# Output gate and silu path of a head side by side in 512 streamed columns

## The chip, the core and the metric

One Trainium2 chip, of which one core runs the kernel. The metric is device time in microseconds (us), the median of several executions. TensorE (PE) does the matmuls; in the profile PEld is its loading of stationary operands, which overlaps with the streaming of others. VectorE is DVE, ScalarE is ACT, GpSimd is POOL, and SP issues the DMA transfers. PSUM, where matmuls accumulate, has banks of 512 fp32 columns for each of 128 partitions.

## The reference, cut to what matters

```python
def reference(x, norm_g, w_in, ..., w_out, final_norm_g):   # x: 1 x 2048 x 1024
    u = rmsnorm(x, norm_g)
    proj = einsum('bsd,de->bse', u, w_in)        # 1024 -> 8200 columns
    (q, k, v, o_pre, z_m, i_pre, f_pre,          # 1024 columns each, gates 4 each
     glu_a, glu_g, z_c) = split(proj)
    hm = mlstm_chunkwise(q, k, v, i_pre + b_i, f_pre + b_f)  # 4 heads of 256
    hm = sigmoid(o_pre) * hm
    hm = headwise_rmsnorm(hm) * mh_norm_g * silu(z_m)
    c = causal_depthwise_conv31(glu_a * sigmoid(glu_g)) + conv_b
    c = silu(layernorm(c)) * silu(z_c)
    return rmsnorm(x + concat(hm, c) @ w_out, final_norm_g)
```

## The kernel before

The 2048 tokens are worked in two halves of 1024 (`hf` 0 and 1). In each half the input projection runs as a row of units (function `unit`, line 321): a unit is one pass over the 1024 input features in 8 k-steps, with four PSUM banks as output, and the pool `gm` has five banks, so a unit starts on the one that the unit before it didn't use. Every product is three matmuls, since both operands are split into a high and a low part (`hi*hi + hi*lo + lo*hi`).

The units of a half follow in the order of the list `seq`: two groups of conv input (`g`), then for each head `v`, `o` (output gate), `z` (silu path), `q`, `k`, and two more `g`; at the end four `c`. Units of kind "fm" (`g`, `q`, `k`, `c`, line 336) hold the weights stationary and stream 512 tokens. Units of kind "tm2" (`v`, `o`, `z`, line 343) hold a tile of 128 tokens stationary and stream 256 weight columns; two token tiles share one bank. Units of kind "tm" (line 350) stream weights too, one token tile to a bank; the output projection at the end uses them with 512 columns.

Weights come by DMA into tiles `wr` of 512 KB (`w_load`, two buffers) and are split in two by `w_prep_`: a copy on ACT (line 221) and a subtraction on POOL (line 222), into four buffers `w`, three tiles ahead of use (`WAHEAD`). For `o` and `z` a split tile holds two k-steps of 256 columns, and starts 48 words into its buffer (`ODD`). So a head's `o` and `z` take 4 loads and 8 splits.

`ev_o` evacuates the output gate with two sigmoids of 256 columns to a bank (line 438), and `ev_z` the silu path with two sigmoids (line 450) and two products on DVE (line 451). Evacuations and weight splits are issued at a high priority (`first_hand`).

The order of instructions on each engine comes from a planner, which places them by priority, readiness and modelled costs. Work behind the units is handed out by two queues at each k-step: `ml_slot` gives out the chunks of the mLSTM of the head before, 26 slots from the unit after `k` on, and `pump` gives out DVE work by credit: the 31 taps of each convolution block (line 787, kept in program order), and in the second half the layernorm of the first.

Of the kernel before, what the change touches and what calls it, by code (L numbers as in the profile page):

```python
# [14 lines left out]
F32 = mybir.dt.float32  # L15
F32R = mybir.dt.float32r
AF = mybir.ActivationFunctionType
ALU = mybir.AluOpType

P = 128  # L20
# [4 lines left out]
HD = 256  # L25
# [14 lines left out]
def hybrid_block_kernel(  # L40
# [12 lines left out]
    nc = tc.nc  # L53
# [5 lines left out]
    PAD, ODD = 8, 48  # L59

    def pool(name, bufs, **kw):
        return ctx.enter_context(tc.tile_pool(name=name, bufs=bufs, **kw))
# [6 lines left out]
    ozp = pool("ozp", 4)  # L69
# [107 lines left out]
    def ml_slot():  # L177
        gate_step()
        if mlq:
            for fn in mlq.popleft():  # L180
                fn()

    def ml_drain():
        while mlq:
            ml_slot()

    def first_hand():
        return tc.high_priority(offset=HP)
# [3 lines left out]
    wsrc = []  # L192
# [4 lines left out]
    def w_load(j):  # L197
        ap, n, _ = wsrc[j]
        r = rp.tile([P, 1056], F32, tag="raw", name=f"wr{j}")
        raws[j] = (r, n)  # L200
        if j > 0:
            with first_hand():
                nc.sync.dma_start(r[:, : 2 * n], ap)

    def w_first(half):
        r, n = raws[0]
# [20 lines left out]
    def w_advance(i):  # L227

        while wstate["prep"] <= min(i + WAHEAD, 2 * len(wsrc) - 1):
            k = wstate["prep"]  # L230
            while wstate["raw"] <= min(k // 2 + 1, len(wsrc) - 1):
                w_load(wstate["raw"])
                wstate["raw"] += 1
            w_prep(k)
            wstate["prep"] += 1
# [6 lines left out]
    rstd = {}  # L242
# [68 lines left out]
    def m_kc(b, kp):  # L311
        with first_hand():
            for j in range(kp, min(kp + 2, 8)):
                if (b, j) not in mraw:
                    m_load(b, j)
            split((f"m{b}", kp), mraw[b, kp])
# [4 lines left out]
    def unit(kind, nk, kpt, ncol, opnd, evac, step_us=2.6, hook=None, toks=None, ntail=0):  # L321


        ps = [gm.tile([P, 512], F32, tag="gm", name=f"gm_{wpos[0]}_{i}") for i in range(4)]
        base = wpos[0]

        def products(kc, i):
            wh, wl = wtile[base + kc // kpt]
            o = (kc % kpt) * ncol
            ah, al = opnd(kc)  # L330
            first, last = kc == 0, kc == nk - 1
            for pi, (wt, at) in enumerate(((wh, ah), (wh, al), (wl, ah))):
                st, sp_ = first and pi == 0, last and pi == 2
                if kind == "fm":
                    cb, tb = i % 2, i // 2
                    nc.tensor.matmul(  # L336
                        ps[i], wt[:, o + cb * P : o + (cb + 1) * P], at[:, tb * 512 : (tb + 1) * 512],
                        start=st, stop=sp_,
                    )
                elif kind == "tm2":  # L340
                    for t2 in range(2):
                        t = 2 * i + t2
                        nc.tensor.matmul(  # L343
                            ps[i][:, t2 * 256 : (t2 + 1) * 256], at[:, t * P : (t + 1) * P],
                            wt[:, o : o + ncol],
                            start=st and t2 == 0, stop=sp_, skip_group_check=True,
                        )
                else:
                    t = toks[i]
                    nc.tensor.matmul(  # L350
                        ps[i][:, :ncol], at[:, t * P : (t + 1) * P], wt[:, o : o + ncol],
                        start=st, stop=sp_,
                    )

        tail = nk - ntail
        for kc in range(tail):
            w_advance(base + kc // kpt)
            if hook is not None:
                hook(kc)
            for i in range(4):  # L360
                products(kc, i)
            ml_slot()
            pump(step_us * PUMP)
        for kc in range(tail, nk):
            w_advance(base + kc // kpt)
        wpos[0] += nk // kpt
        for i in range(4):
            for kc in range(tail, nk):
                products(kc, i)
            if hook is not None:  # L370
                for kc in range(tail + i * ntail // 4, tail + (i + 1) * ntail // 4):
                    hook(kc)
            with first_hand():
                evac(i, ps[i])
            for _ in range(ntail // 4):
                ml_slot()
                pump(step_us * PUMP)


    q_t, k_t, v_t, oz_t = {}, {}, {}, {}  # L380
# [50 lines left out]
            )  # L431
        return f

    def ev_o(hf, h):
        def f(i, ps):
            oz_t[h, i] = ozp.tile([P, 2, 2, HD], F32, tag="oz", name=f"oz_{hf}_{h}_{i}")
            for j in range(2):
                nc.scalar.activation(
                    oz_t[h, i][:, 0, j], ps[:, j * HD : (j + 1) * HD], AF.Sigmoid,
                    scale=rstd["c"][:, 2 * i + j : 2 * i + j + 1],  # L440
                )
        return f

    def ev_z(hf, h):
        def f(i, ps):
            t = oz_t[h, i]
            for j in range(2):
                pv = ps[:, j * HD : (j + 1) * HD]
                rc = rstd["c"][:, 2 * i + j : 2 * i + j + 1]
                nc.scalar.activation(t[:, 1, j], pv, AF.Sigmoid, scale=rc)  # L450
                nc.vector.scalar_tensor_tensor(  # L451
                    out=t[:, 1, j], in0=pv, scalar=rc, in1=t[:, 1, j], op0=ALU.mult, op1=ALU.mult
                )
        return f

    def gates(hf, gt):
# [450 lines left out]
    WID = {}  # L907
    n = 0
# [12 lines left out]
    for hf in range(2):  # L921
        s = [("g", 0)]
        for h in range(NH):
            s += [("v", h)] + ([("g", 1)] if h == 0 else []) + [("o", h), ("z", h), ("q", h), ("k", h)]
            if h < 3:
                s += [("g", 2 * h + 2), ("g", 2 * h + 3)]
        s += [("c", j) for j in range(4)]
        seq.append(s)
        for u in s:
            if u == ("v", 0):  # L930
                for _ in range(2):
                    for g in range(2):
                        wsrc.append((wv0[g], 528, 0))
            else:
                for g in range(2):
                    wsrc.append((wu[WID[u], g], 512, ODD if u[0] in "ozv" else 0))
    for b in range(4):
        for nn in range(2):
            for g in range(8):
# [18 lines left out]
    for hf in range(2):  # L958
        gt = gp.tile([P, NCH, 8], F32, tag="g_gt", name=f"gt{hf}")
        key = f"u{hf}"  # L960

        def opnd(kc, key=key):
            return uh[key, kc], ul[key, kc]

        s = seq[hf]
        hold[0] = 10**6
        for ui, (nm, i) in enumerate(s):
            hook = None
            if ui == len(s) - 1:
                if hf == 0:  # L970
                    def hook(kc):
                        if kc >= 1:
                            u_kc(1, kc - 1)
                else:
                    def hook(kc):
                        if kc >= 1:
                            m_kc(0, kc - 1)
            if nm == "g":
                unit("fm", 8, 2, 256, opnd, ev_glu(hf, i), hook=hook)
            elif nm == "c":  # L980
                unit("fm", 8, 2, 256, opnd, ev_zc(hf, i), hook=hook)
            elif nm == "q":
                unit("fm", 8, 2, 256, opnd, ev_q(hf, i), hook=hook)
            elif nm == "k":
                unit("fm", 8, 2, 256, opnd, ev_k(hf, i), hook=hook)
                mlstm(hf, i)
            elif nm == "o":
                unit("tm2", 8, 2, 256, opnd, ev_o(hf, i), hook=hook)
            elif nm == "z":
                unit("tm2", 8, 2, 256, opnd, ev_z(hf, i), hook=hook)  # L990
            elif i > 0:
                unit("tm2", 8, 2, 256, opnd, ev_v(hf, i), hook=hook)
            else:
                for g in range(2):
                    unit("tm", 8, 2, 264, opnd, ev_v0(hf, g, gt), step_us=1.35, toks=[4 * g + i for i in range(4)])
                gq.append([0, gates(hf, gt)])
                gate_step()
        if hf == 0:
            u_kc(1, 7)
            u_rstd(1)  # L1000
        else:
            m_kc(0, 7)
        if hf == 1:
            ml_drain()
            drain()
        for blk in range(4):
            layernorm(hf, blk)
# [36 lines left out]
    for b in range(4):  # L1044
        if b == 2:
            drain()
        for nn in range(2):
            hook = None
# [78 lines left out]
```

## Time and profile before

| what | value |
|---|---|
| median of 3 runs | 2008.14 us (2007.59 to 2011.28) |
| the profiled execution | 2014.07 us |
| its span, first to last instruction | 2012.4 us |
| mean granted TensorE clock | 0.993 |
| PE busy | 1975.9 us, 98% |
| DVE busy | 1445.4 us, 72% |
| ACT busy | 827.7 us, 41% |
| POOL busy | 792.3 us, 39% |

The profile is that of one execution. An engine's busy time is the union of its instructions' times; matmuls overlap one another in it. A wait is put down to the instruction that released it.

### The profile page before, as it was taken

How to read it: one execution, taken by the hardware profiler on the slowest of the kernel's cores; microseconds unless marked ns; L12 is line 12 of the kernel's file. 1: busy time of each engine (PE TensorE's matmuls, PEld its weight loads, DVE VectorE, ACT ScalarE, POOL GpSimd, SP SyncE). 2: the span in 40 equal slices, each digit the busy share in tenths (PEclk: the TensorE clock that was granted, in tenths of full speed). 3: DMA queues.
4: the chain of work that ended last, by engine and by line, in shares of the span. 5: the costliest groups of instructions: out<-in, count | busy, mean ns of one | idle time of the engine just before them, and what ended most of it. 6: DMA issues, size and time to landing. Idle time of an engine off the chain costs nothing.

```text
span 2012.4 us, 29602 instructions
## 1 busy us (share of the span) xinstructions
PE 1975.9 (98%) x11562; PEld 1744.7 (87%) x11562; DVE 1445.4 (72%) x1915; ACT 827.7 (41%) x1703; POOL 792.3 (39%) x740
## 2 busy tenths in 40 slices
PE   8999999999999999999999999999999999999998
PEld 7998998899899888888889879988998887788887
DVE  6598887699679765557799998977896658733221
ACT  5233432442343246545345224424523555543332
POOL 4632432333243332433333324333432236565564
PEclk9999999999999999999999999999999999999999
DMA  4121121212122233335211211211221566766452
GB/s 151 64 69 53 58 74 43 63 49 74 42 69 74 74 110 125 113 126 162 85 53 53 69 42 59 74 53 53 64 74 53 163 220 200 248 231 231 155 190 95
DMA packets 85836, 204.10 MB, mean 101 GB/s; under 512 B 7296, under 2 KB 40256, under 8 KB 85696
## 3 DMA queue, kind: packets, MB, share of 16 engines
q1 hardware_dynamic: 85696, 202.21, 30.6%
q8 instruction: 91, 1.49, 0.3%
q14 instruction: 49, 0.40, 0.1%
HBM read 159.15 MB, written 43.03 MB: 100 GB/s over the span
## 4 chain that ended last, share of the span: by engine, by line
PE 73%; DVE 18%; DMA 3%; issue 2%; ACT 2%; POOL 0%; SPq 0%; POOLq 0%; DVEq 0%; ACTq 0%
PE gm L336 32%; PE gm L343 18%; PE gm L350 16%; DVE y L787 11%; PE num L601 3%; PE kv L601 2%; PE sk L627 1%; DMA ly<-ysc 1%; DVE sm L302 1%; DMA wr<-in_wo 1%; PE mt L714 1%; DVE ly L844 1%; DMA ysc<-y 1%; PE sk L631 1%; ACT ly L881 0%
## 5 line engine op out<-in xcount | busy, mean ns | idle before, releaser
L222 POOL TENSOR_TENSOR w<-wr,w 128x512 fp32r<-128x512 f32 (+1 forms) x392 | 603.1, 1543 | 878.2 <-ACT w L221 859.4
L336 PE MATMUL gm<-u_u,w 128*128 128x512 f32 x3840 | 908.6, 392 | 0.7 <-DVE u_u L293 0.6
L336 PEld LDWEIGHTS gm<-u_u,w 128*128 128x128 f32 x3840 | 712.5, 188 | 143.2 <-DVE u_u L293 1.3
L787 DVE SCALAR_TENSOR_TENSOR y<-c,vec,y 128x1024 f32<-128x1024 f32 x480 | 714.5, 1489 | 9.7
L343 PE MATMUL gm<-w,u_u 128*128 128x256 f32 x4224 | 521.9, 281 | 5.7 <-DVE oz L451 3.4
L343 PEld LDWEIGHTS gm<-w,u_u 128*128 128x128 f32 x4224 | 505.8, 190 | 7.6 <-DVE oz L451 3.6
L221 ACT CAST w<-wr 128x512 fp32r<-128x512 f32 (+1 forms) x392 | 241.4, 620 | 591.6 <-PE gm L336 200.2
L350 PE MATMUL gm<-w,u_m 128*128 128x512 f32 x1536 | 355.0, 392 | 3.1 <-POOL w L222 1.9
L350 PEld LDWEIGHTS gm<-w,u_m 128*128 128x128 f32 x1536 | 289.1, 189 | 64.2 <-POOL w L222 2.8
L281 DVE TENSOR_TENSOR u_m<-mr,u_m 128x1024 fp32r<-128x1024 f32 x32 | 47.2, 1475 | 77.7 <-ACT u_m L280 77.7
L1019 DVE TENSOR_TENSOR ht<-gm,ht 128x512 f32<-128x512 f32 x32 | 21.5, 687 | 112.2 <-PE gm L350 112.2
L700 POOL TENSOR_TENSOR ss<-ss,nhalf 128x1 f32<-128x1 f32 x64 | 55.5, 867 | 111.9 <-ACT sq L699 111.3
L633 DVE SCALAR_TENSOR_TENSOR w<-sk,rs,ee 128x128 f32<-128x128 f32 x64 | 22.0, 344 | 81.6 <-PE sk L631 79.1
L601 PE MATMUL kv<-v,kw 128*128 128x258 f32 x360 | 74.3, 291 | 0.6 <-DVE cs L666 0.4
L666 DVE SCALAR_TENSOR_TENSOR cs<-cs,g_so,kv 128x258 f32<-128x258 f32 x112 | 53.3, 476 | 25.1 <-PE kv L601 24.7
L639 ACT ACTIVATE kw<-sk,g_wa 128x256 fp32r<-128x256 f32 x60 | 28.3, 472 | 81.7 <-DVE w L633 81.6
L719 ACT ACTIVATE mo<-mt,vec 128x128 f32<-128x128 f32 x128 | 39.7, 362 | 52.3 <-PE mt L714 52.1
L601 PEld LDWEIGHTS kv<-v,kw 128*128 128x128 f32 x360 | 56.9, 190 | 3.2 <-DVE cs L666 0.6
L408 DVE SCALAR_TENSOR_TENSOR v<-gm,rs,v 128x256 fp32r<-128x256 f32 x64 | 29.5, 475 | 33.4 <-ACT v L407 33.4
L699 ACT ACTIVATE sq<-hm 128x257 bf16<-128x257 f32 x64 | 26.9, 420 | 64.6 <-DVE hm L694 64.4
L761 POOL TENSOR_TENSOR c<-c,g 128x512 f32<-128x512 f32 x32 | 40.9, 1284 | 30.4 <-ACT g L760 27.6
L350 PE MATMUL gm<-w,u_u 128*128 128x264 f32 x384 | 50.8, 294 | 0.0
(200 smaller groups left out, 1818.0 us busy)
## 6 DMA issues: line engine op xcount, KB each, us to landing
wr<-in_wu SPq DMA_DIRECT2D x123, 512.0 KB, 3.6
wr<-in_wo SPq DMA_DIRECT2D x64, 512.0 KB, 3.6
mr<-mixs SPq DMA_DIRECT2D x32, 512.0 KB, 4.6
ysc<-y SPq DMA_DIRECT2D x16, 512.0 KB, 2.6
mixs<-mo SPq DMA_DIRECT2D x32, 256.0 KB, 2.1
zsc<-zc SPq DMA_DIRECT2D x32, 256.0 KB, 2.1
ly<-ysc SPq DMA_DIRECT2D x16, 512.0 KB, 5.2
lz<-zsc SPq DMA_DIRECT2D x16, 512.0 KB, 6.0
```

What stands on the lines that cost most here:

```text
L221: nc.scalar.copy(hi, s)
L222: nc.gpsimd.tensor_tensor(out=lo, in0=s, in1=hi.bitcast(F32), op=ALU.subtract)
L281: nc.vector.tensor_tensor(out=l_, in0=src, in1=h_.bitcast(F32), op=ALU.subtract)
L336: nc.tensor.matmul(ps[i], wt[:, o + cb * P : o + (cb + 1) * P], at[:, tb * 512 : (tb + 1) * 512], start=st, stop=sp_,)
L343: nc.tensor.matmul(ps[i][:, t2 * 256 : (t2 + 1) * 256], at[:, t * P : (t + 1) * P], wt[:, o : o + ncol], start=st and t2 == 0, stop=sp_, s ...
L350: nc.tensor.matmul(ps[i][:, :ncol], at[:, t * P : (t + 1) * P], wt[:, o : o + ncol], start=st, stop=sp_,)
L601: nc.tensor.matmul(ps, x_, y_, start=start and i == 0, stop=stop and i == 2)
L666: nc.vector.scalar_tensor_tensor(out=cs[:, d], in0=cs[:, d], scalar=so[:, h, c : c + 1], in1=kv[:, :VW], op0=ALU.mult, op1=ALU.add,)
L700: nc.gpsimd.tensor_tensor(out=ss, in0=ss, in1=nhalf[:, 0:1], op=ALU.pow)
L719: nc.scalar.activation(mo[:, d, (cc % 2) * P : (cc % 2 + 1) * P], mt[:, d * P : (d + 1) * P], AF.Identity, scale=col(V_MG, 2 * h + d),)
L761: nc.gpsimd.tensor_tensor(out=c[:, sl], in0=c[:, sl], in1=g, op=ALU.mult)
L787: tc.keep_in_program_order(nc.vector.scalar_tensor_tensor(out=y, in0=c[:, j + i * H2 : j + (i + 1) * H2], scalar=col(V_CW, b * CW + j), in1=y,
```

## The change

The units `o` and `z` of a head become two units `oz` of kind "tm", each with four token tiles. A weight tile now holds one k-step of 256 `o` columns and 256 `z` columns side by side, so a matmul streams 512 columns into a whole bank that belongs to one token tile. Both units go through all the weights of the head, so they are loaded and split twice. A load is made of two DMA transfers, one from the `o` weights and one from the `z` weights, interleaved in the destination. A bank is evacuated by one sigmoid over both halves and one product on DVE for the `z` half. The offset `ODD` is left for `v` alone.

```diff
@@ w_load
-                nc.sync.dma_start(r[:, : 2 * n], ap)
+                if isinstance(ap, tuple):
+                    rv = r[:, :1024].rearrange("p (a b c) -> p a b c", a=2, b=2)
+                    for k in range(2):
+                        nc.sync.dma_start(rv[:, :, k, :], ap[k])
+                else:
+                    nc.sync.dma_start(r[:, : 2 * n], ap)
@@ evacuation
-    def ev_o(hf, h):
...
-    def ev_z(hf, h):
...
+    def ev_oz(hf, h, g):
+
         def f(i, ps):
+            t = 4 * g + i
+            if t % 2 == 0:
+                oz_t[h, t // 2] = ozp.tile([P, 2, 2, HD], F32, tag="oz", name=f"oz_{hf}_{h}_{t // 2}")
+            o = oz_t[h, t // 2][:, :, t % 2, :]
+            rc = rstd["c"][:, t : t + 1]
+            nc.scalar.activation(o, ps.rearrange("p (a b) -> p a b", a=2), AF.Sigmoid, scale=rc)
+            nc.vector.scalar_tensor_tensor(
+                out=o[:, 1], in0=ps[:, HD : 2 * HD], scalar=rc, in1=o[:, 1], op0=ALU.mult, op1=ALU.mult
+            )
         return f
@@ order of units and of weights
-            s += [("v", h)] + ([("g", 1)] if h == 0 else []) + [("o", h), ("z", h), ("q", h), ("k", h)]
+            s += [("v", h)] + ([("g", 1)] if h == 0 else []) + [("oz", h), ("q", h), ("k", h)]
...
+            elif u[0] == "oz":
+                for _ in range(2):
+                    for g in range(2):
+                        for k in (0, 2):
+                            wsrc.append((
+                                tuple(wu[WID[nm, u[1]], g][:, k : k + 2, :] for nm in "oz"), 512, 0
+                            ))
             else:
                 for g in range(2):
-                    wsrc.append((wu[WID[u], g], 512, ODD if u[0] in "ozv" else 0))
+                    wsrc.append((wu[WID[u], g], 512, ODD if u[0] == "v" else 0))
...
-            elif nm == "o":
-                unit("tm2", 8, 2, 256, opnd, ev_o(hf, i), hook=hook)
-            elif nm == "z":
-                unit("tm2", 8, 2, 256, opnd, ev_z(hf, i), hook=hook)
+            elif nm == "oz":
+                for g in range(2):
+                    unit("tm", 8, 1, 512, opnd, ev_oz(hf, i, g), hook=hook, toks=[4 * g + j for j in range(4)])
```

## Rows read from the trace of the kernel before

**Rows 1.** The page: busy time of the engines, and DVE in 40 slices.
```profile
PE 1975.9 (98%) x11562; PEld 1744.7 (87%) x11562; DVE 1445.4 (72%) x1915; ACT 827.7 (41%) x1703; POOL 792.3 (39%) x740
...
DVE  6598887699679765557799998977896658733221
```

**Rows 2.** Groups by line and shape: busy us, mean ns | idle before, releasers.
```profile
L787 DVE SCALAR_TENSOR_TENSOR y<-c,vec,y 128x1024 f32<-128x1024 f32 x480 | 714.5, 1489 | 9.7
L222 POOL TENSOR_TENSOR w<-wr,w 128x512 fp32r<-128x512 f32 x376 | 577.9, 1541 | 859.0 <-ACT w L221 844.5 <-DVE dn L687 9.4 <-DVE c1l L592 4.6
...
L221 ACT CAST w<-wr 128x512 fp32r<-128x512 f32 x376 | 231.4, 619 | 577.4 <-PE gm L336 189.3 <-PE gm L350 114.0 <-issue 111.8
...
L450 ACT ACTIVATE oz<-gm,rs 128x256 f32<-128x256 f32 x64 | 27.9, 478 | 37.6 <-PE gm L343 23.4 <-DVE oz L451 14.2
...
L438 ACT ACTIVATE oz<-gm,rs 128x256 f32<-128x256 f32 x64 | 25.8, 486 | 9.8 <-PE gm L343 6.9 <-DVE hm L706 2.8
```

**Rows 3.** Timeline of PE, three undisturbed stretches: start us, us, instructions.
```profile
284.28 23.40 PE L343 MATMUL gm<-w,u_u 128*128 128x256 f32 x205
...
635.74 22.66 PE L343 MATMUL gm<-w,u_u 128*128 128x256 f32 x191
...
1786.67 131.63 PE L350 MATMUL gm<-w,u_m 128*128 128x512 f32 x580
```

**Rows 4.** Windows, line 343 alone: the sum over the eight o-and-z stretches.
```profile
sum 399.00, PE 374.36 PEld 365.13; mean PE 46.79 PEld 45.64
```

**Rows 5.** Waits of PE: who for whom, us in total, times, longest us.
```profile
PE gm L343 <- DVE oz L451: 3.4, 1, 3.4
...
PE gm L350 <- POOL w L222: 1.9, 2, 1.2
...
PE gm L343 <- ACT oz L438: 1.7, 2, 1.1
```

**Rows 6.** Timeline of PE, first head of the second half, z.
```profile
928.26 5.92 PE L343 MATMUL gm<-w,u_u 128*128 128x256 f32 x26 [3.42 <-DVE oz L451]
```

**Rows 7.** Windows: length, busy us of each engine, granted clock, DMA share, GB/s.
```profile
881.30:937.20 55.90, 51.40 (x408) 50.76 (x407) 35.54 (x43) 28.38 (x50) 15.28 (x10) 0.94 0.49 153
...
985.00:1206.00 221.00, 209.67 (x1266) 185.79 (x1265) 211.60 (x263) 79.81 (x181) 75.07 (x67) 0.98 0.17 54
...
1830.90:1874.40 43.50, 43.50 (x194) 36.05 (x193) 10.80 (x10) 13.22 (x26) 26.83 (x24) 1.00 0.62 216
```

**Rows 8.** The chain that ended last, 970 to 1195 us: two taps, and its end.
```profile
977.71 1.29 DVE y L787
...
980.35 2.21 DVE y L787
...
1192.67 2.56 PE gm L336 x6
```

**Rows 9.** Timeline of all engines where z of head 3 ends, first half.
```profile
656.31 0.47 ACT L450 ACTIVATE oz<-gm,rs 128x256 f32<-128x256 f32 x1 [2.87 <-PE gm L343]
...
658.23 8.12 PE L336 MATMUL gm<-u_u,w 128*128 128x512 f32 x35
...
658.84 0.87 DVE L451 SCALAR_TENSOR_TENSOR oz<-gm,rs,oz 128x256 f32<-128x256 f32 x2
...
659.49 1.29 POOL L222 TENSOR_TENSOR w<-wr,w 128x512 fp32r<-128x512 f32 x1 [4.29 <-ACT w L221]
659.63 2.23 DVE L787 SCALAR_TENSOR_TENSOR y<-c,vec,y 128x1024 f32<-128x1024 f32 x1
```

**Rows 10.** DMA issues: KB each, median us to landing.
```profile
wr<-in_wu SPq DMA_DIRECT2D x123, 512.0 KB, 3.6
...
mixs<-mo SPq DMA_DIRECT2D x32, 256.0 KB, 2.1
```

**Rows 11.** Source views of lines 451 and 787: ns min/median/max, first and last start.
```profile
L451 DVE SCALAR_TENSOR_TENSOR oz<-gm,rs,oz x64: 467/475/485, 134.5 to 1490.4; 128x256 f32<-128x256 f32 x64
...
L787 DVE SCALAR_TENSOR_TENSOR y<-c,vec,y x480: 1250/1285/2415, 82.6 to 1579.0; 128x1024 f32<-128x1024 f32 x160
```

More of the change, by code (lines that the diff above doesn't have):

```diff
@@ L432, in ev_v0 @@
         return f
-    def ev_o(hf, h):
+    def ev_oz(hf, h, g):
         def f(i, ps):
[L436 to L442, printed above, removed]
-    def ev_z(hf, h):
[L445 to L453, printed above, removed]
+            t = 4 * g + i
[7 more added lines that the diff above has]
+            )
         return f
```

## The prediction

> **What bounds the kernel now.** I read the page's busy line and slices first [rows 1]. TensorE (PE) is busy 98% of the span, VectorE (DVE) 72%, the others under half; so the end is set by the stream of matmuls, and DVE matters only where its slices stand at 9 and PE waits for it. The list of groups [rows 2] then gives durations of what an edit on ACT, POOL and DVE costs. A matmul's own duration is no use as a price, because matmuls overlap: the price is the step from start to start, which the timeline of PE gives where one line runs undisturbed [rows 3]. A row of n matmuls lasts n-1 steps and the last one's own time (0.28 us for 256 columns, 0.39 us for 512). So the 205 of the first row step by (23.40-0.28)/204 = 113.3 ns, the 191 of the second by (22.66-0.28)/190 = 117.8 ns (three more z units have that same row), and the 580 of 512 columns, streamed weights against stationary tokens just as the change wants it, by (131.63-0.39)/579 = 226.7 ns.
>
> **The stream of the output gate and silu units (o, z).** Before, a head takes 2 x 192 matmuls of 256 columns, after, 2 x 96 of 512: the same columns. At the faster old step a head is 384 x 113.3 = 43.5 us, at the slower 384 x 117.8 = 45.2 us; after, 192 x 226.7 = 43.5 us. Eight heads (four in each half) so gain between 0 and 8 x 1.7 = 13.9 us. The slow step is in four of the five undisturbed z stretches, while o and the disturbed z units are mixed with other matmuls; I take five eighths of the way, about 8.5 us. As a check, line 343 is busy 374.4 us in the eight stretches together [rows 4], against 8 x 43.5 = 348: 26 us is the most that could go, with every wait and every tail between pieces.
>
> The Trainium skill, "TensorE: Matmul & The Clock Gate", section "Back-to-back issue gap", gives a warm isolated matmul N/2.4 + 2.5 ns. By it 256 columns would step by 109.2 and 512 by 215.8 ns, and an estimate from that page for the gain is 1536 x 2.6 = 4 us in place of 8.5. Both traced steps are longer than the page's, so the sum goes by the rows.
>
> **The waits of PE in these units.** PE waited 3.4 and 1.7 us there for the evacuations of lines 451 and 438 [rows 5], nearly all in the first head of the second half. The long one was followed by 26 matmuls in 5.92 us [rows 6], (5.92-0.28)/25 = 226 ns each where 117 is usual: the granted clock of that stretch is 0.94 [rows 7], so part of it ran at the lower of the clock's two levels, 1.2 GHz, for another 2.8 us. That is 7.9 us in all. It is caused by layernorm work of the first half on ACT and DVE, which the change leaves in place; I credit 2 us, with 0 and 7.9 as ends.
>
> **Weights.** Each head's o and z weights are now split twice, once for each unit: 8 more copies on ACT and 8 more subtractions on POOL in a head, 64 in all: 64 x 0.619 = 40 us of ACT and 64 x 1.541 = 99 us of POOL [rows 2]. Neither engine is near full, and the output projection already runs at this rate: 16 splits in 43.5 us, with PE busy 43.5 of 43.5 [rows 7]. So supply costs nothing where DVE and ACT are quiet; where they weren't, PE waited 1.9 us for POOL in the whole projection [rows 5]. The loads double too, 32 to 64 transfers' worth, each now in two issues of 256 KB in 1 KB pieces. The nearest row of that form is the store of mo, 2.1 us from issue to landing, against 3.6 us for one 512 KB load [rows 10]; two are 2.1 to 4.2 us plus an issue. A pair of weight tiles lasts 2 x 12 x 0.2267 = 5.4 us, and three tiles are ready ahead, so the transfer stays covered. If SP held one up behind a layernorm store, that cover would shrink from the 17 us of now to 8. Cost taken: 0.
>
> **Evacuation.** The o units took 8 sigmoids of 0.486 us, the z units 8 of 0.478 [rows 2]; 8 of 512 wide take their place, between 0.48 and 0.96 us each, near the 0.619 of the 512-wide copy. ACT is relieved by some 2 to 3 us a head, off the path. DVE keeps its 8 products of 0.475 us [rows 11], but now the first unit's banks wait for DVE as well, where o's waited for ACT alone. What stands in front is a convolution tap. In [rows 9] the first sigmoid of z ends at 656.78 and its DVE product starts at 658.84, 2.1 us late; q streamed from 658.23 on without a pause, because with five banks it starts on the free one and can go up to eight k-steps deep on four ready weight tiles. In the new pair a tile holds one k-step: four tiles give 4 x 3 x 0.2267 = 2.7 us on the free bank. The first bank is finished 2.04 us before the unit ends, and sigmoid, lateness and product take 0.6 + 2.1 + 0.5 = 3.2 us, so it is back 1.2 us into the next unit, within the 2.7. One lengthened tap (2.2 us) in front of it makes 3.4 and PE waits 0.7. Ends: 0, and 8 x 2.2 = 17.6 us; I take 0.3 us a head, 2.4 us.
>
> **What POOL does to DVE.** A tap alone takes about 1.285 us, and the mean of all is 1.489 [rows 2, 11]. In [rows 9] the tap of 659.63 meets a POOL subtraction of 659.49 and takes 2.23; so also the chain's 2.21 against its neighbour's 1.29 [rows 8]. One collision costs DVE 0.92 us; spread over the splits that run beside taps, 480 x (1.489-1.285) = 98 us over the 376 + 16 - 128 = 264 splits ahead of the projection is 0.37 each. Eight more a head are 3.0 to 7.4 us of DVE. In most heads DVE has room for it in the k unit. It hasn't from 985 to 1206 us, where it is busy 211.6 of 221 us [rows 7] and where the chain runs tap by tap from 974 until PE takes over at 1192 [rows 8]: the second half's second head. There I take 5 us, and the 1.1 us of faster stream in that head is lost, being off the path. Ends: 0, and 14.7 us if the next head carries the lateness too.
>
> The Trainium skill, "GPSIMD Engine Reference", section "Key points", says that GpSimd shares its SBUF interfaces with VectorE and contends with instructions that have two SBUF inputs. The trace agrees: the tap, with two, spans 1.250 to 2.415 us, while the product of line 451, with one input in PSUM, stays within 0.467 and 0.485 [rows 11]. That rule speaks against the change.
>
> **Sum.** -8.5 (stream) -2 (waits) +2.4 (banks) +5 +1.1 (DVE) = -2 us. The profiled execution took 2014.07 us (span 2012.4 and 1.7 around it), 5.9 us over the median 2008.14 of the three timed runs; so 2012.1 in its own terms, 2006 on the median.
>
> **Rivals.** *The stream's gain is kept.* The new order takes the waits away and DVE finds room: -8.5 - 7.9 = -16.4, 1992 us. For it: in most o and z units PE never waits now. Against: the DVE chain of 218 us.
> *DVE becomes the bound.* The place is the second half, heads two and three; the price 14.7 us for 16 collisions at 0.92, 8 x 0.7 us at the banks, less 8.5 us of stream: +12, 2020 us. It decides once a head's extra DVE time exceeds what k leaves idle. For it: 211.6 of 221 busy. Against: not every split meets a tap. This is the contention rule of the Trainium skill at full price.
> *The stream is not faster at all.* If the old step is mostly 113.3 ns, what is left of the sum is -2 + 2.4 + 5 = +5.4: 2013.5 us. For it: the first row of [rows 3]. Against: the four rows at 117.8.
>
> **How the numbers follow.** A measurement tells about 0.2% (4 us) from no change. Forecast (2006, own range 2000 to 2012): 0.42, of which 0.14 faster, 0.22 same, 0.06 slower. Gain kept: 0.22, faster. DVE the bound: 0.25, of which 0.23 slower, 0.02 same. No faster stream: 0.11, of which 0.05 same, 0.06 slower. So faster 0.36, same 0.29, slower 0.35. Half of each outer case lies beyond its centre, so the range goes from 1991 to 2022.
>
> **What would show it.** Rows of 512-column matmuls in the new units stepping by 227 ns; some 43.5 us for a pair that nothing interrupts; 64 more splits; taps of 2.2 us at nearly twice the rate inside the pairs; PE waiting for line 451's successor at the middle of a pair by under 1 us; the DVE chain after 974 longer by about 5 us. Wrong if PE waits for POOL's weights inside the pairs, if mid-pair waits reach 2 us, or if the planner's new order moves waits in stages that the diff doesn't touch by more than these few microseconds.

## The result and the profile after

The changed kernel takes 2080.19 us (2078.94 to 2081.9, four runs) against 2007.87 for the kernel before beside it: a ratio of 1.0358, 95% interval 1.0341 to 1.0375. It is 72 us slower, where 2 us faster was forecast, and far beyond the range's upper end of 2022. Its profiled execution has a span of 2077.7 us and a mean granted clock of 0.977 (before: 2012.4 and 0.993).

In the changed kernel the copy of a weight split is line 226 and the subtraction 227, the matmuls of `oz` are line 355, those of `q` and `k` 341, of `v` 348, sigmoid and product of `oz` 447 and 448, the taps 784, and the evacuation of a `g` unit 753 (c) and 756 (gate).

The page of the changed kernel, busy time, DVE's and the clock's slices, three groups and two rows of DMA issues (to set against [rows 1, 2, 10]):
```profile
PE 1982.1 (95%) x10026; PEld 1676.1 (81%) x10026; DVE 1496.5 (72%) x1915; ACT 853.4 (41%) x1702; POOL 906.8 (44%) x804
...
DVE  6698887799689766467789977996886766833122
...
PEclk9999999999999999979998999999999999999999
...
L227 POOL TENSOR_TENSOR w<-wr,w 128x512 fp32r<-128x512 f32 (+1 forms) x456 | 721.0, 1589 | 807.9 <-ACT w L226 791.8
...
L784 DVE SCALAR_TENSOR_TENSOR y<-c,vec,y 128x1024 f32<-128x1024 f32 x480 | 750.5, 1564 | 9.6
...
wr<-in_wu SPq DMA_DIRECT2D x91, 512.0 KB, 3.5
wr<-in_wu SPq DMA_DIRECT2D x130, 256.0 KB, 3.0
```
PE's busy time has hardly moved (6 us more), and its share has fallen from 98 to 95%: the added time is PE standing still. DVE does the same 1915 instructions in 51 us more. POOL has its 64 more splits.

The waits of PE in the changed kernel (against [rows 5]):
```profile
PE lv L856 <- DVE lq L825: 20.4, 3, 11.9
PE gm L341 <- DVE oz L448: 13.3, 7, 4.5
PE gm L355 <- DVE oz L448: 9.5, 6, 3.4
...
PE lm L833 <- DVE ls L825: 7.0, 3, 5.3
PE bc_l L274 <- DVE dg_l L270: 4.9, 4, 1.6
PE gm L355 <- POOL w L227: 4.0, 5, 1.2
```
Two things are new: PE waits 22.8 us in all for the DVE product of `oz` (second and third row), and 32 us for layernorm's own steps (the `lv`, `lm` and `bc_l` rows). The latter mislead on their own: a tiny matmul of layernorm is named because nothing else on PE can run. Of the 4.0 us for POOL's split weights, 1.9 are in the output projection, as before [rows 5]; some 2 us are new, inside the pairs.

Where the time goes shows best unit by unit. The table is worked out from the timelines of PE: from the first matmul of a head's `o` (or `oz`) to the first of its `q`, in us, for the four heads of each half (1.0 to 1.3 is the first half, 2.0 to 2.3 the second). The runs below `after` are the experiments of the next section.

| kernel | 1.0 | 1.1 | 1.2 | 1.3 | 2.0 | 2.1 | 2.2 | 2.3 |
|---|---|---|---|---|---|---|---|---|
| before | 47.0 | 47.5 | 49.9 | 49.9 | 55.9 | 52.7 | 48.1 | 48.1 |
| after | 50.6 | 48.7 | 50.2 | 50.2 | 90.3 | 72.5 | 50.9 | 47.5 |
| x5_pool | 53.4 | 48.5 | 50.4 | 50.4 | 58.3 | 59.9 | 51.4 | 48.7 |
| x1_depth | 46.3 | 47.0 | 48.9 | 48.9 | 92.6 | 65.0 | 46.5 | 48.7 |
| x9_nosub | 46.3 | 47.5 | 50.2 | 50.2 | 91.0 | 70.1 | 45.5 | 46.7 |
| x11_depth_dg | 46.3 | 47.0 | 48.9 | 48.9 | 48.7 | 67.0 | 46.3 | 48.7 |

Two pairs carry most of it: the first head of the second half, 34 us longer, and the second, 20 us longer. The first half as a whole loses 11.0 us. Between the two long pairs 12 us are made up again, and from the last head's `q` to the `c` units another 7 are lost. (The profiled execution before is 6 us over its median, so these sums come to 65 us and not to 72.)

The timeline of PE in the first of them, and below it DVE's and POOL's of the same stretch (against [rows 6], where PE streams on):
```profile
892.27 7.42 PE L355 MATMUL gm<-w,u_u 128*128 128x512 f32 x32
...
899.88 1.19 PE L355 MATMUL gm<-w,u_u 128*128 128x512 f32 x4
...
903.61 0.67 PE L833 MATMUL lm<-ls,ones 128*128 128x256 f32 x2 [0.45 <-DVE ls L825]
916.18 0.98 PE L856 MATMUL lv<-invd,lq 128*128 128x1 f32 x4 [11.90 <-DVE lq L825]
...
938.76 7.55 PE L355 MATMUL gm<-w,u_u 128*128 128x512 f32 x24
```
```profile
936.77 0.42 DVE L270 TENSOR_TENSOR dg_l<-ident,lrs 128x256 f32<-128x256 f32 x1 [0.88 <-POOL lrs L859]
937.11 1.28 DVE L756 TENSOR_TENSOR g<-gm,rb 128x512 f32<-128x512 f32 x2
```
```profile
893.22 1.55 POOL L227 TENSOR_TENSOR w<-wr,w 128x512 fp32r<-128x512 f32 x1 [4.87 <-ACT w L226]
...
941.63 2.28 POOL L227 TENSOR_TENSOR w<-wr,w 128x512 fp32r<-128x512 f32 x1
```
PE does 32 + 4 = 36 matmuls of `oz` and then none for 37.7 us. Thirty-six is 3 banks x 4 weight tiles x 3 products: the unit has used up every split tile on every bank that it holds. Its fourth bank, and one for the unit after it, are still full with the gates of the `g` unit before, which DVE takes out at 937.11, right behind the third diagonal of layernorm in its order. Until then no weight tile can be released, since the fourth bank has still to use all four, and so POOL splits nothing from 893 to 941. In the kernel before the gates come out just as late, at 938.99; there four tiles hold all eight k-steps of a unit, and PE went on with what it had.

The second head has the same, behind other work. PE of the changed kernel:
```profile
1109.62 5.17 PE L355 MATMUL gm<-w,u_u 128*128 128x512 f32 x22
...
1115.20 0.73 PE L355 MATMUL gm<-w,u_u 128*128 128x512 f32 x2
...
1134.09 4.46 PE L355 MATMUL gm<-w,u_u 128*128 128x512 f32 x12 [1.38 <-DVE v L413]
1139.65 3.04 PE L355 MATMUL gm<-w,u_u 128*128 128x512 f32 x12 [1.11 <-DVE c L753]
```
22 + 2 = 24 is two banks by 4 tiles by 3. Then the third bank comes when DVE has evacuated `v`, the fourth with a `c` of the `g` unit, each good for 12 more.

Windows of the changed kernel over the two pairs and over the stretch of the DVE chain (columns and the old stretches in [rows 7]):
```profile
892.30:982.60 90.30, 56.93 (x235) 43.52 (x234) 62.04 (x77) 48.70 (x79) 30.93 (x23) 0.79 0.48 154
985.00:1206.00 221.00, 202.48 (x1023) 170.18 (x1022) 194.82 (x230) 73.91 (x161) 87.78 (x73) 0.94 0.20 64
1109.60:1182.20 72.60, 56.80 (x229) 44.00 (x228) 71.27 (x70) 22.69 (x50) 41.29 (x30) 0.84 0.24 80
```
In the second head's pair DVE is busy 71.27 of 72.60 us; in the first head's only 62 of 90, so there it is the order of the work and not its amount.

### The profile page after: what moved, and what is told of

Same layout as the page of the kernel before. It is cut to its first block, busy times and chain, and to the rows that moved or that the text cites. A ratio compares the mean times of both kernels' runs of the same rounds, so it can differ in the third digit from the quotient of the medians.

```text
span 2077.7 us, 26869 instructions
## 1 busy us (share of the span) xinstructions
PE 1982.1 (95%) x10026; PEld 1676.1 (81%) x10026; DVE 1496.5 (72%) x1915; ACT 853.4 (41%) x1702; POOL 906.8 (44%) x804
## 4 chain that ended last, share of the span: by engine, by line
PE 69%; DVE 21%; DMA 3%; issue 3%; ACT 3%; POOL 2%; SPq 0%; POOLq 0%; ACTq 0%; DVEq 0%
PE gm L341 37%; PE gm L355 20%; DVE y L784 13%; PE gm L348 5%; PE num L598 3%; PE kv L598 2%; PE sk L624 1%; DMA ysc<-y 1%; DMA ly<-ysc 1%; POOL w L227 1%; DVE oz L448 1%; DVE ly L841 1%; POOL ss L697 1%; DMA wr<-in_wo 1%; PE sk L628 1%
## 5 line engine op out<-in xcount | busy, mean ns | idle before, releaser
L227 POOL TENSOR_TENSOR w<-wr,w 128x512 fp32r<-128x512 f32 (+1 forms) x456 | 721.0, 1589 | 807.9 <-ACT w L226 791.8
L784 DVE SCALAR_TENSOR_TENSOR y<-c,vec,y 128x1024 f32<-128x1024 f32 x480 | 750.5, 1564 | 9.6
L226 ACT CAST w<-wr 128x512 fp32r<-128x512 f32 (+1 forms) x456 | 280.3, 620 | 687.6 <-PE gm L341 279.1
L355 PE MATMUL gm<-w,u_u 128*128 128x512 f32 (+1 forms) x1920 | 424.1, 377 | 14.2 <-DVE oz L448 9.5
L355 PEld LDWEIGHTS gm<-w,u_u 128*128 128x128 f32 x1920 | 337.0, 192 | 78.3 <-DVE oz L448 12.2
L348 PE MATMUL gm<-w,u_u 128*128 128x256 f32 x1152 | 145.9, 278 | 1.6 <-DVE g L756 0.9
L348 PEld LDWEIGHTS gm<-w,u_u 128*128 128x128 f32 x1152 | 138.6, 188 | 2.3 <-DVE g L756 1.1
L716 ACT ACTIVATE mo<-mt,vec 128x128 f32<-128x128 f32 x128 | 39.8, 362 | 50.3 <-PE mt L711 50.2
```

What stands on the lines that cost most here:

```text
L226: nc.scalar.copy(hi, s)
L227: nc.gpsimd.tensor_tensor(out=lo, in0=s, in1=hi.bitcast(F32), op=ALU.subtract)
L348: nc.tensor.matmul(ps[i][:, t2 * 256 : (t2 + 1) * 256], at[:, t * P : (t + 1) * P], wt[:, o : o + ncol], start=st and t2 == 0, stop=sp_, s ...
L355: nc.tensor.matmul(ps[i][:, :ncol], at[:, t * P : (t + 1) * P], wt[:, o : o + ncol], start=st, stop=sp_,)
L716: nc.scalar.activation(mo[:, d, (cc % 2) * P : (cc % 2 + 1) * P], mt[:, d * P : (d + 1) * P], AF.Identity, scale=col(V_MG, 2 * h + d),)
L784: tc.keep_in_program_order(nc.vector.scalar_tensor_tensor(out=y, in0=c[:, j + i * H2 : j + (i + 1) * H2], scalar=col(V_CW, b * CW + j), in1=y,
```

## The experiments

Two theories stood. *Depth*: a weight tile that holds one k-step lets a unit run ahead by free banks x 4 k-steps only, and banks that were held late at no cost now stop PE. *Contention*: the 64 more subtractions on POOL lengthen DVE's instructions, and DVE comes late with everything. Medians in us, ratios to the kernel before measured beside each:

| run | base and edit | median | ratio, 95% interval |
|---|---|---|---|
| x1_depth | before, `o` and `z` weight tiles of one k-step | 2054.71 | 1.0229, 1.0212 to 1.0247 |
| x2_twice | before, `o` and `z` splits done twice | 2043.83 | 1.0177, 1.0157 to 1.0197 |
| x5_pool | before, only POOL's part of it twice | 2043.67 | 1.0173, 1.0158 to 1.0188 |
| x6_act | before, only ACT's part of it twice | 2011.08 | 1.0014, 1.0005 to 1.0023 |
| x7_before_act | before, `z` banks released by ACT | 2008.01 | 0.9993, 0.9984 to 1.0003 |
| x4b_dg | before, layernorm's diagonals in another pool | 2015.15 | 1.0040, 1.0025 to 1.0054 |
| x11_depth_dg | x1_depth and x4b_dg | 2024.91 | 1.0076, 1.0056 to 1.0095 |
| x9_nosub | after, without the added subtractions | 2047.40 | 1.0191, 1.0176 to 1.0206 |
| x3_act | after, `oz` banks released by ACT | 2054.15 | 1.0231, 1.0212 to 1.0249 |
| x4_dg | after, layernorm's diagonals in another pool | 2080.75 | 1.0360, 1.0340 to 1.0379 |
| x34 | x3_act and x4_dg | 2053.42 | 1.0228, 1.0213 to 1.0243 |
| x10_nosub_dg | x9_nosub and x4_dg | 2042.76 | 1.0164, 1.0142 to 1.0187 |
| x8_c | after, smaller buffers (control) | 2112.72 | 1.0515, 1.0497 to 1.0532 |
| x8_d | x8_c, six weight tiles | 2102.61 | 1.0465, 1.0450 to 1.0481 |

**Depth alone, in the kernel before (x1_depth).** Same columns, streams and units; only the weight tiles are halved.
```diff
-                    wsrc.append((wu[WID[u], g], 512, ODD if u[0] in "ozv" else 0))
+                    if u[0] in "oz":
+                        for k in (0, 2):
+                            wsrc.append((wu[WID[u], g][:, k : k + 2, :], 256, ODD))
...
-                unit("tm2", 8, 2, 256, opnd, ev_o(hf, i), hook=hook)
+                unit("tm2", 8, 1, 256, opnd, ev_o(hf, i), hook=hook)
```
(and the same for `z`)

> The kernel before, with one thing of the change: an o or z weight tile holds one k-step of 256 columns instead of two (same columns loaded and split, in twice as many pieces of half the size; the 256-column stream and the old evacuations stay). Theory A, depth times banks (PE stops because only four k-steps of split weights are ready while banks are held): a good part of the 72 us comes back, 2040 to 2070 us, with the stop in the second half's first head. Rival B, the doubled split work and its collisions with DVE: the work is about that of before, so 2003 to 2018 us. Rival C, doubled loads: also 2003 to 2018.

It costs 45 us. The pair of the second half's first head is 37 us longer (92.6 for 55.9), 10 of these are made up before the next pair, and that one is 12 longer (65.0 for 52.7). PE's timeline in the first:
```profile
886.11 5.34 PE L343 MATMUL gm<-w,u_u 128*128 128x256 f32 x44
...
891.66 3.43 PE L343 MATMUL gm<-w,u_u 128*128 128x256 f32 x28
...
908.54 0.98 PE L859 MATMUL lv<-invd,lq 128*128 128x1 f32 x4 [12.18 <-DVE lq L828]
...
931.09 5.00 PE L343 MATMUL gm<-w,u_u 128*128 128x256 f32 x33
```
44 + 28 = 72 matmuls, 3 banks x 4 tiles x 3 products x 2 token tiles in a bank, and then the same standstill. Depth makes the stop, without the wide stream and without one added column of split work. The doubled loads of the change were not tested alone. ACT's waits for the input weights rose with them:
```profile
ACT w L226 <- DMA wr<-in_wu: 60.5, 20, 7.3
```
Before, these were 2.6 us; in x9_nosub below they are 21.8, with the same loads. Of PE's waits in the changed kernel only the 4.0 us for split weights are put down to weights.

**The second split alone (x2_twice, x5_pool, x6_act).** Both instructions of the `o` and `z` splits are issued twice, then only the subtraction, then only the copy.
```diff
-        nc.gpsimd.tensor_tensor(out=lo, in0=s, in1=hi.bitcast(F32), op=ALU.subtract)
+        for _ in range(2 if len(wsrc[i // 2]) > 3 else 1):     # o and z entries carry a fourth field
+            nc.gpsimd.tensor_tensor(out=lo, in0=s, in1=hi.bitcast(F32), op=ALU.subtract)
```

> The kernel before, with each o and z weight tile split twice over (64 more ACT copies and 64 more POOL subtractions, the second writing the same values), at the old depth of two k-steps in a tile. Theory A, depth times banks: 2006 to 2018 us. Rival B, split work and DVE collisions: most of the loss shows, 2045 us or more.

> The kernel before, with only the POOL subtraction of each o and z weight tile made twice (64 more on POOL, none on ACT). If the 34 us of the run that doubled the whole split are POOL's collisions with DVE: 2030 to 2045 us. If they are the extra copies in ACT's queue: 2005 to 2018.

> The kernel before, with only ScalarE's copy of the o and z weight splits done twice (64 more copies of 0.62 us, no more subtractions). If the cost of a second split lies with GpSimd's subtractions, as the run with those alone says: 2003 to 2014 us. If ScalarE's copies carry part of it: 2018 or more.

Twice both costs 1.77% (2043.83 us, just under the range given for contention), twice the subtraction 1.73%, twice the copy 0.14%: the second split costs some 35 us, and nearly all of it is POOL's. The page of x5_pool, busy time and the taps:
```profile
PE 1979.4 (97%) x11562; PEld 1743.1 (85%) x11562; DVE 1496.3 (73%) x1915; ACT 827.3 (41%) x1703; POOL 909.6 (45%) x804
...
L788 DVE SCALAR_TENSOR_TENSOR y<-c,vec,y 128x1024 f32<-128x1024 f32 x480 | 738.7, 1539 | 9.7
```
DVE's 1915 instructions take 1496.3 us for 1445.4 [rows 1]: 51 us for 64 subtractions, 0.80 each. The taps carry 24 of it (480 x 0.050). The rest lies in other instructions that work in SBUF alone; those that read PSUM took 318 us in all before and 0.5 less in x5_pool. PE's waits go up by 26 us: 16 for DVE, 6 for ACT and 4 for POOL itself. The time is lost all along: 16.8 us by the start of the first half's `c` units, 29.1 by the end (profiled executions compared); the pairs of the first head in the first half and the second in the second take 53.4 for 47.0 and 59.9 for 52.7.

**The added subtractions taken out of the changed kernel (x9_nosub).**
```diff
+        if len(wsrc[i // 2]) > 3:      # second oz unit of a head
+            lo = hi
+        else:
+            nc.gpsimd.tensor_tensor(out=lo, in0=s, in1=hi.bitcast(F32), op=ALU.subtract)
```

> The changed kernel, but the second oz unit of each head takes the high part of the weights in place of the low part, so the 64 added subtractions on GpSimd are gone (the low part's product is computed with wrong numbers; matmuls, loads and ScalarE's copies stay). If the added subtractions cost what they cost when put into the kernel before (about 30 to 35 us): 2040 to 2055, and the mean tap goes from 1.564 back to about 1.50. If the stop at the held banks covers them, so that the two causes overlap: 2058 to 2075. The stop of about 35 us in the second half's first head stays in either case, because a weight tile still holds one k-step.

33 us come back, and the first half is as long as before to 0.2 us. The page and PE's waits of x9_nosub:
```profile
PE 1972.4 (96%) x10026; PEld 1672.0 (82%) x10026; DVE 1446.7 (71%) x1915; ACT 854.9 (42%) x1702; POOL 789.9 (39%) x740
```
```profile
PE lv L859 <- DVE lq L828: 19.9, 3, 11.4
...
PE gm L358 <- DVE oz L451: 3.5, 3, 1.6
...
PE gm L344 <- DVE oz L451: 0.4, 1, 0.4
```
DVE is back at 1446.7 us, the waits for the product at 3.9 from 22.8, and the stop stands (91.0 us in the first pair). So the 72 us are 33 that go with the subtractions and 39 that stay without them.

**Who releases the banks (x3_act, x7_before_act).** ACT takes sigmoid and scaled z out of the bank; the silu is made from SBUF, and 64 DVE products go. x7_before_act does the same to `z` of the kernel before.
```diff
-            nc.scalar.activation(o, ps.rearrange("p (a b) -> p a b", a=2), AF.Sigmoid, scale=rc)
-            nc.vector.scalar_tensor_tensor(
-                out=o[:, 1], in0=ps[:, HD : 2 * HD], scalar=rc, in1=o[:, 1], op0=ALU.mult, op1=ALU.mult
-            )
+            nc.scalar.activation(o[:, 0], ps[:, :HD], AF.Sigmoid, scale=rc)
+            nc.scalar.activation(o[:, 1], ps[:, HD : 2 * HD], AF.Identity, scale=rc)
+            if i == 3:
+                for p in (2 * g, 2 * g + 1):
+                    zz = oz_t[h, p][:, 1]
+                    nc.scalar.activation(zz, zz, AF.Silu)
```

> The changed kernel, but a bank is released by ACT alone: sigmoid of the o half, a scaled copy of the z half, and a silu of the z halves from SBUF once per unit; the 64 DVE products go. PE's 22.8 us of waits for those products, and the low clock behind them, should go if they are a term of their own: 2040 to 2060 us. If the loss is all in the second half's first head (banks held by a g unit behind the layernorm), little changes: 2070 to 2080.

> The kernel before, with z evacuated by ACT alone (a scaled copy of 256 columns from the bank, then silu from SBUF at the end of the unit); the 64 DVE products of 0.475 us go. If the second half hangs on DVE's chain of taps, as the chain says, part of the 30 us comes back as time: 1990 to 2004 us. If PE's stream alone sets the end: 2005 to 2012.

In the changed kernel 26 us come back, in the kernel before nothing (0.9993, the interval includes 1). The taps stay long in x3_act (1.556 us mean). So a DVE release is harmless where DVE is on time. That the subtractions make DVE late, and the release by DVE passes that on to PE, fits both; but x3_act also takes 64 products of 0.475 us off DVE, and no run separates this from the release. x3_act and x9_nosub were not tried together.

**More weight tiles (x8_c, x8_d).** Six tiles fit only with smaller ones and with two buffers fewer in a pool that the mLSTM and layernorm use; x8_c is that alone, as a control.
```diff
-    k4p = pool("k4p", 7)
+    k4p = pool("k4p", 5)
...
-        both = wp.tile([P, 1152], F32R, tag="w", name=f"w{i}")
+        both = wp.tile([P, 1072], F32R, tag="w", name=f"w{i}")
```
```diff
-    wp = pool("wp", 4)
+    wp = pool("wp", 6)
...
-    WAHEAD = 3
+    WAHEAD = 5
```

> Control: the changed kernel with five 4 KB buffers in the pool of q, k and the layernorm instead of seven, and weight buffers cut from 1152 to 1072 words, still four of them and three tiles ahead. Somewhat slower than the changed kernel if the layernorm wants its buffers: 2075 to 2110 us under every theory.

> The control with six weight buffers and five tiles ahead: six k-steps of ready weights instead of four. Theory A, depth times banks: 15 to 40 us below the control, above all in the second half's first two heads. Rival B, split work and DVE collisions alone: within 5 us of the control.

The control came out 3 us above its range. Six tiles gave 10 us, less than *depth* had expected and more than its rival. The timeline of PE in x8_d says why:
```profile
898.90 7.59 PE L355 MATMUL gm<-w,u_u 128*128 128x512 f32 x32
...
906.69 5.33 PE L355 MATMUL gm<-w,u_u 128*128 128x512 f32 x22
...
961.70 13.44 PE L355 MATMUL gm<-w,u_u 128*128 128x512 f32 x48
```
32 + 22 = 54 = 3 banks x 6 tiles x 3, just as the count predicts, but the banks are held until 961: two more tiles are some 4 us of work against a hold of tens. By the count the unit would have to run as deep as a whole unit, as the old tiles let it; that was not tried.

**The hold itself (x4_dg, x34, x4b_dg, x10_nosub_dg, x11_depth_dg).** The gates of the `g` unit stand behind layernorm's diagonals on DVE, both being in the pool `k2p`. With the diagonals in a pool of their own the gates come out early.
```diff
-        dg = k2p.tile([P, 4, P], F32, tag="k2", name=f"dg_{nm}")
+        own = nmp if nm[0] == "l" else k2p
+        dg = own.tile([P, 4, P], F32, tag="nm" if nm[0] == "l" else "k2", name=f"dg_{nm}")
```

> The changed kernel, but the layernorm's diagonal tile takes its buffer from another pool than the g units' gate tile, so two banks of the second half's second g unit come free before the layernorm chain instead of after it. Theory A: the pair of that head falls from 90 us to 50 to 60, 2040 to 2055 us in all. Rival B, split work and DVE collisions: no change, 2073 to 2085.

> The changed kernel with both earlier edits: banks released by ScalarE alone (64 VectorE products gone, the silu taken from SBUF) and the first half's layernorm diagonals in a pool of their own, so that the two g banks come free early. The first edit alone gave -26 us, the second alone 0, because VectorE became the bound behind it. If VectorE's work is what eats the second edit's gain, the 64 products fewer let part of it show: 2025 to 2045 us. If the two edits only add (-26 and 0): 2050 to 2058. If the stop at the held banks costs nothing whatever else is done: over 2050 too, with the lag coming back in the second half's first three heads.

> The kernel before, with the first half's layernorm diagonals in a pool of their own, as in the run on the changed kernel. There the edit made layernorm end later (1012 against 975 to 980 us). If that lateness is the edit's own price, it shows here too: 2015 to 2040 us, layernorm ending after 990. If it came from the changed kernel's crowded VectorE: 2003 to 2014.

> The changed kernel without the 64 added subtractions on GpSimd (the second oz unit takes the weights' high part in place of the low part, as in the run before this one) and with the layernorm diagonals in a pool of their own. The run without the subtractions took 2047, with the stop of 34.5 us in place. If that stop is the banks that layernorm holds, and the second edit gained nothing before only because GpSimd's added work crowded VectorE: the stop goes and stays gone, 2010 to 2025 us. If the time under the stop is used by VectorE, so that removing it only moves the wait: 2038 to 2055, the lag coming back from q on in the second half's first two heads.

> The kernel before with o and z weight tiles of one k-step (2055 us alone, 46 over before) and the layernorm diagonals in a pool of their own. No subtraction is doubled in columns: 128 half-wide ones stand for 64. If the depth's cost is the held banks: 2010 to 2025 us. If the stop only gives VectorE time that it needs: 2038 to 2055. If what costs is the second hold, v and c behind the mLSTM in the next head, which this edit leaves: 2025 to 2038.

In every one the long stop in the first head is gone (x4_dg 52.9 us, x34 48.4, x10_nosub_dg 53.4, x11_depth_dg 48.7), and yet the changed kernel gains hardly anything by it: x4_dg 0, though its pair falls as *depth* had said; x34 under 1 against x3_act; x10_nosub_dg 5 against x9_nosub. With the tiles of x1_depth it gains 30 (2054.71 to 2024.91). The difference is layernorm. DVE's waits from 880 to 1000 us, x10_nosub_dg first, then x11_depth_dg:
```profile
DVE lrs L862 <- PE lv L860: 21.4, 4, 8.1
```
```profile
DVE lrs L862 <- PE lv L860: 5.8, 3, 3.1
```
And PE between the same two matmuls of layernorm (second mean, second variance), again x10_nosub_dg and then x11_depth_dg:
```profile
898.03 0.59 PE L837 MATMUL lm<-ls,ones 128*128 128x256 f32 x2
898.27 8.92 PE L359 MATMUL gm<-w,u_u 128*128 128x512 f32 x36
910.47 11.98 PE L359 MATMUL gm<-w,u_u 128*128 128x512 f32 x39 [3.28 <-ACT w L226]
922.29 0.50 PE L860 MATMUL lv<-invd,lq 128*128 128x1 f32 x4
```
```profile
897.03 0.60 PE L837 MATMUL lm<-ls,ones 128*128 128x256 f32 x2
897.28 15.78 PE L344 MATMUL gm<-w,u_u 128*128 128x256 f32 x136
912.89 0.50 PE L860 MATMUL lv<-invd,lq 128*128 128x1 f32 x4
```
The same two matmuls are 24.3 us apart here against 15.9. Little of that is their place in PE's order: 75 matmuls of 512 columns stand between, for 136 of 256. PE also stands still for 3.3 us until ACT has copied a weight tile, and then runs slowly. The windows show it, first the whole of layernorm's four rounds (first mean to last broadcast) in x10_nosub_dg and the 6 us after that stop, then the four rounds in x11_depth_dg (columns as in [rows 7]):
```profile
876.80:986.90 110.10, 99.58 (x423) 79.72 (x422) 59.54 (x78) 55.60 (x87) 30.16 (x22) 0.92 0.47 150
...
910.50:916.60 6.10, 6.10 (x15) 4.78 (x16) 2.34 (x3) 1.82 (x2) 0.00 (x0) 0.50 0.90 288
```
```profile
879.90:970.80 90.90, 89.79 (x597) 81.57 (x596) 59.28 (x78) 50.15 (x92) 33.64 (x28) 1.00 0.51 161
```
Layernorm takes 19 us longer. Nine of these are PE standing still (10.5 us for 1.1), the longest time 6.3 us for `q` banks that ACT has still to empty; the granted clock is 0.92 for 1.00, and 0.50 behind the first stop, the lower of its two levels (1.2 GHz); and 17 more matmuls of `q` and `k`, some 4 us, stand in between. DVE is equally busy in both, 59 us. So with the long hold gone the changed program stops at shorter ones. Layernorm's last product starts at 995.6 us in x10_nosub_dg, 978.0 in x11_depth_dg, 1012 in x4_dg; the convolution waits for that, and between the first head's `q` and the second's the lag comes back (in x10_nosub_dg from -2 to +36 us against before, 20 of it in the second head's pair). The contention that I had expected to be the cause of this is not: x10_nosub_dg has no added subtractions. Nor is it the edit, which costs 7 us by itself, with layernorm's last product at 979 (x4b_dg). Which of the changed program's other differences brings the shorter stops (the 64 more copies on ACT, the doubled loads, banks that wait for ACT and DVE, or the planner's order) was not tried, so how much of the 39 us is depth alone in the changed kernel stays open.

In x11_depth_dg the first hold is gone, and 14 us remain, as much as the second head's pair is longer (67.0 for 52.7): the hold behind `v` and `c`, which this edit leaves.

## Why the prediction was wrong

**Weights, "supply costs nothing": wrong, and the largest step.** The prediction counted the copies, subtractions and transfers, whose supply did hold (PE's waits for POOL's weights went from 1.9 to 4.0 us, the 256 KB loads land in 3.0). It saw, too, that a tile holds one k-step, but used that only for the middle of a pair, where a bank is 1 to 3 us late. It didn't ask how long the banks of the *previous* units are held, and so took for free what the old tiles covered: a `g` unit's gates held to 939 us, `v` and `c` keeping PE from the weights' next use for 18 us in the next head (1116 to 1134). Price taken 0; measured 45 us where the small tiles alone were put into the kernel before, and 39 in the changed kernel without the added subtractions, which holds all the rest of the change too. PE also waited some 2 us for POOL's weights inside the pairs, one of the signs of being wrong. [Rows 6] lay in that very stretch and showed PE running through it.

**What POOL does to DVE: the mechanism right, the size too small.** Predicted 5 us, at most 14.7; 33 in the changed kernel, 35 in the kernel before. Two terms of it failed. A subtraction costs DVE 0.80 us and not 0.37: for the taps the 0.37 was right (24.2/64 = 0.38 in x5_pool), but DVE's other instructions, which carry more than half, were left out. And it was charged to one head only, where DVE is full for 220 us; x5_pool loses 16.8 us in the first half, where DVE's slices have room on average and the evacuations still come late. The rule of the Trainium skill that was weighed there ("GPSIMD Engine Reference", "Key points") pointed the right way: x5_pool and x9_nosub bear it out. The rival built on it, DVE as the bound at 2020, had the mechanism, but with 16 collisions at 0.92 in two heads where 64 subtractions at 0.80 in eight were to be counted.

**Banks, "0.3 us a head": 22.8 us of waits** for the product. Inside the pairs they reach 3.4 us at once, where 2 was named as a sign of being wrong, and at the start of `q` 4.5. Nearly all of it goes with the subtractions (3.9 us without them).

**The stream, "-8.5": about right, but eaten by waits.** The new step is near what was forecast. The timeline of PE in an undisturbed stretch of the changed kernel:
```profile
468.73 23.17 PE L355 MATMUL gm<-w,u_u 128*128 128x512 f32 x101
```
(23.17 - 0.39)/100 = 227.8 ns, against 226.7. The `o` units, left aside as mixed, have the slow old step in places too, as two rows of the kernel before show:
```profile
93.42 12.41 PE L343 MATMUL gm<-w,u_u 128*128 128x256 f32 x103
...
1453.96 6.52 PE L343 MATMUL gm<-w,u_u 128*128 128x256 f32 x54
```
They give 118.9 and 117.7 ns. Over all `o` and `z` units the undisturbed steps average 116.2 ns by their start times, just the five eighths that were guessed, and with 227.8 after that is 7 us for the eight heads. It didn't reach the end: in the two least disturbed heads the pair went from 49.9 to 50.2 us, since the 1.0 us of faster steps goes where the mLSTM's matmuls in the pair now wait for DVE (twice, 0.95 us together in the third head of the first half), and a little more besides. In x9_nosub the last head's pair is shorter than before (46.72 us for 48.06), by as much as the steps say. The rival "the stream is not faster at all" rested on an old step of mostly 113.3 ns, which the trace doesn't have.

**The waits, "-2":** in the first head of the second half they went up, by the stop.

Right were both steps of the stream, the doubled load and split work, the taps' part of the contention and its sign. The sum failed since its two costs that matter came at 0 and 5 us instead of 39 and 33.

## What to carry to other kernels

Before a weight tile is made to hold fewer k-steps, count how far a unit can run ahead, free banks x ready tiles x matmuls that each allows, and set that against how long the units in front hold their banks in the trace, also where no wait shows today: a late release that costs nothing may be covered by this depth alone. Work added to an engine that is 39% busy is not free if it lengthens another's instructions: price it by the busy time of that other engine in a run with only this work doubled. And when a stop is removed without a gain, follow the next chain of small dependent instructions through the engine that was stopped, and count in the trace what stands between them: work, further stops, and time at the low clock.

## What the runs showed of the hardware

64 more POOL subtractions of 128x512 fp32, 1.54 us each in the kernel before, lengthened DVE's unchanged 1915 instructions by 51 us, 0.80 us each (x5_pool), and 64 more ACT copies of the same tiles by nothing (x6_act: DVE busy 1437.1 us). All of it is in instructions that work in SBUF alone: the 64 products of `oz`, which read PSUM, keep their 475 ns, at most 485 before and 486 in x5_pool.

The long pauses of PE cost more than their length here. After the one in the second head, in which PE was busy 7.1 of 18.1 us, 12 matmuls took 4.46 us (1134.09) at a granted clock of 0.65, between its two levels of 1.2 and 2.4 GHz, where the next 12 took 3.04 (1139.65) at 1.00; in the window of the first pair the clock is 0.79.

Not explained: the old 256-column step was near 118 ns in some stretches of `o` and `z` and 113.5 in others of the same shape, and in x11_depth_dg it was 113.3 in the third head's `z` (207 matmuls in 23.62 us from 459.73), where the kernel before had 117.8.
